# A two-layer decoder trunk on one core: adding the last overflow tile of the last layer in PSUM, and a second norm without GpSimd

## The chip, the cores and the metric

One core of a Trainium2 chip runs the whole program. The metric is the device time of one execution in microseconds, the median of several runs; lower is better.

## What is computed

Two layers over 512 positions of width 1024, batch 1. Each layer mixes the positions (layer 0 with a gated recurrence and a state-space model, layer 1 with two kinds of attention), normalises, sends every position to two of 16 SwiGLU experts, and normalises again. The change touches what stands at the end of each layer:

```python
x = layer_norm(DN_ALPHA * x + mix, ln1_g[layer], ln1_b[layer])
ffn = hier_moe(x, ...)        # sum over two experts e of gate[t, e] * expert_e(x[t])
x = layer_norm(DN_ALPHA * x + ffn, ln2_g[layer], ln2_b[layer])

def layer_norm(x, g, b):
    mu = mean(x, axis=-1); var = mean(square(x - mu), axis=-1)
    return (x - mu) * rsqrt(var + 1e-5) * g + b
```

The input and the result are 512 x 1024 float32.

## The kernel before

Tokens are rows, in four blocks of 128 partitions. The expert stage (`moe`, L1636) works on tiles of 128 tokens: one tile for each of the 16 experts, then up to NOV = 7 overflow tiles for experts that got more than 128 tokens. Every tile is gathered from the buffer `x1d` in memory (`gather`, L1571, an indirect DMA of GpSimd), goes through the expert's two products (`gate_up`, `hidden`, `hiddenT`, `down`), is scaled by its gate on ScalarE (L1616) and is added by a scattering DMA of GpSimd (L1617) to the buffer `yd` in memory, which starts as DN_ALPHA times x. Products in float32 are made of three products of rounded parts (`hilo`, L194 to L196: ScalarE writes the rounded part, VectorE the rest; `mm3`, L198 to L202).

Each of the seven overflow tiles stands in a branch, `with tc.If(nov > o)` (L1746). Every engine passes each branch by itself. On the way past a branch that isn't taken an engine only brings its semaphores up to where the branch would have left them; GpSimd does that with an instruction of its own for the semaphores of its DMAs (INC_SWDGE_SEM). With these inputs layer 0 takes four of the seven branches and layer 1 takes one.

After the branches the four blocks of 128 tokens of `yd` are read back on SyncE's queue (L1752) into `row` tiles. That read waits for the scatters and for GpSimd to be past all the branches. Then comes the second norm of the four blocks: `stats` on VectorE (L290, L1766), `scale` (the inverse root in some eleven tiny VectorE instructions for two blocks at a time, L266 to L281), and `norm`, which splits the columns: the lower 512 go through two VectorE instructions (L1782, L1784), the upper 512 through ScalarE (L1778), GpSimd (L1779, and L1781 for the first two blocks) and VectorE (L1787, for the last two). `weave` interleaves the generators, so the order on each engine is the order in which they are written. `finish` is called for each block: in layer 0 `odd_token` (L1289), which stores the block, transposes it on TensorE, splits it by `hilo` and multiplies it with the key and value weights of layer 1; in layer 1 only the DMA to the output (L1824).

Of the kernel before, what the change touches and what calls it, by code (L numbers as in the profile page):

```python
# [20 lines left out]
L = 512  # L21
# [141 lines left out]
class Trunk:  # L163
# [60 lines left out]
    def consts2(self):  # L224
        nc, c = self.nc, self.cst

        self.lt = c.tile([128, 128], BF, name="lt")
        self.iof = c.tile([128, 128], F32, name="iof")
        f = c.tile([128, 128], F32, name="ltf")
        nc.gpsimd.memset(f, 1.0)  # L230
        nc.gpsimd.affine_select(out=f, in_=f, compare_op=ALU.is_gt, fill=0.0, base=0,
                                pattern=[[1, 128]], channel_multiplier=-1)
        nc.gpsimd.tensor_copy(self.lt, f)
        self.onesf = c.tile([128, 128], F32, name="onesf")
        nc.gpsimd.memset(self.onesf, 1.0)
# [8 lines left out]
        nc.gpsimd.iota(bid, pattern=[[128, 4]], base=-8192, channel_multiplier=0,  # L244
                       allow_small_or_imprecise_dtypes=True)

        self.Q = c.tile([128, 8, 5], BF, name="Q")
# [15 lines left out]
        q.dma_start(bt, b.rearrange("(o d) -> o d", o=1).to_broadcast([128, D]))  # L263
        self.lnp = gt, bt

    def rsqrt_steps(self, z, var, n, pool, eps=1e-5):  # L266

        V = self.nc.vector
        t = lambda nm, dt=F32: pool.tile([128, n], dt, name="rq" + nm, bufs=4)
        h, m, y = t("h"), t("m"), t("i", I32)  # L270
        V.tensor_scalar(h, var, eps, 0.5, op0=ADD, op1=MUL)
        yield 1
        V.tensor_scalar(y, h.bitcast(I32), -0.5, float(0x5f3759df - 0x400000 - 0x80000000), op0=MUL, op1=ADD)
        y = y.bitcast(F32)
        for i in range(3):
            yield 1
            V.tensor_mul(m, y, y)
            yield 1
            V.tensor_mul(m, m, h)
# [763 lines left out]
    def wo_finish(self, layer, x):  # L1043
# [2 lines left out]
        V = nc.vector  # L1046
        res, mv, sts, rs = [], [], [], []
        for tt in range(NT):
            r = mo.tile([128, D], F32, name="row", bufs=6)
            if layer == 0:  # L1050
                nc.sync.dma_start(r, x[blk(tt), :])
            res.append(r)
# [550 lines left out]
        self.hilo(tp[:, :256], ht[:, 0], ht[:, 1])  # L1603
        return ht

    def down(self, s, ht, W):
        nc, mo = self.nc, self.mo
        ys = mo.tile([128, D], F32, name="row", bufs=6)
# [8 lines left out]
        return lambda: self.scattered(s, nc.gpsimd.indirect_dma_start(out=self.yd, out_offset=bass.IndirectOffsetOnAxis(ap=self.toki[:, s:s + 1], axis=0),  # L1617
                                     in_=ys, in_offset=None, bounds_check=L - 1, oob_is_err=False, compute_op=ADD))

    def after(self, inst, *before):  # L1620
        for b in before:
# [14 lines left out]
    def moe(self, layer, lg, between, start, before, after, finish):  # L1636
# [19 lines left out]
        def products(s, qs, xt):  # L1656
            nonlocal c, hp
            if qs[0] == 0:
                hp = self.acc()
            for q in qs:  # L1660
                self.gate_up(hp, xt, q, *self.chunk(c))
                c += 1
        hp = None
        products(0, (0, 1), xt)
        xn = self.xgT(ORD[1])
# [3 lines left out]
        for e in range(NEXP):  # L1669
# [78 lines left out]
        rows = []  # L1748
        mv = mo.tile([128, NT, 2], F32, name="bnmv4", bufs=1)
        for tt in range(NT):  # L1750
            r = mo.tile([128, D], F32, name="row", bufs=6)
# [4 lines left out]
        rs = mo.tile([128, NT], F32, name="lnrs", bufs=1)  # L1756
        nm = mo.tile([128, NT], F32, name="lnnm", bufs=1)
        g, b = self.lnp
        lo, hi = blk(0, 512), blk(1, 512)
        sts = [mo.tile([128, 2, 6], F32, name="bnst", bufs=4) for _ in range(NT)]  # L1760

        def stats(tt):
            for h in range(2):
                self.ln_stats(sts[tt], rows[tt], h)
                yield 1
            V.bn_aggr(mv[:, tt, :], sts[tt])  # L1766
            yield 1

        def scale(q):
            s = blk(q, 2)  # L1770
            yield from self.rsqrt_steps(rs[:, s], mv[:, s, 1], 2, mo)
            yield 1
            V.scalar_tensor_tensor(nm[:, s], mv[:, s, 0], -1.0, rs[:, s], op0=MUL, op1=MUL)
            yield 1

        def norm(tt):
            r = rows[tt]
            nc.scalar.activation(r[:, hi], r[:, hi], AF.Identity, scale=rs[:, tt:tt + 1], bias=nm[:, tt:tt + 1])  # L1778
            nc.gpsimd.tensor_mul(r[:, hi], r[:, hi], g[:, hi])  # L1779
            if tt < 2:  # L1780
                nc.gpsimd.tensor_add(r[:, hi], r[:, hi], b[:, hi])  # L1781
            V.scalar_tensor_tensor(r[:, lo], r[:, lo], mv[:, tt, 0:1], g[:, lo], op0=SUB, op1=MUL)  # L1782
            yield 1
            V.scalar_tensor_tensor(r[:, lo], r[:, lo], rs[:, tt:tt + 1], b[:, lo], op0=MUL, op1=ADD)  # L1784
            yield 1
            if tt >= 2:
                V.tensor_add(r[:, hi], r[:, hi], b[:, hi])  # L1787
            finish(tt, r)
            yield 1

        def each(f, *i):
            for j in i:
                yield from f(j)
        run_all(each(stats, 0, 1))
        weave(each(stats, 2, 3), scale(0))
        weave(each(norm, 0, 1), scale(1))
        run_all(each(norm, 2, 3))

    def run(self):
        nc, tc, I = self.nc, self.tc, self.I  # L1800
# [4 lines left out]
        for layer in range(2):  # L1805
# [5 lines left out]
            with ExitStack() as em:  # L1811
                self.mo = em.enter_context(tc.tile_pool(name="mo", bufs=2))
                self.rx = em.enter_context(tc.tile_pool(name="rxp", bufs=4))
                self.xg = []
                for i in range(4):
                    self.xg.append(self.mo.tile([128, D], F32, name=f"xg{i}", bufs=1))
                st.ahead_load = 4
# [41 lines left out]
```

## Time and profile before

| | us |
|---|---|
| median of 3 runs | 1006.04 (1003.46 to 1008.68) |
| the profiled execution, its own time | 1003.56 |
| its span in the profile | 1001.9 |
| TensorE matmul busy | 845.2 (84%) |
| VectorE busy | 789.1 (79%) |
| ScalarE busy | 566.4 (57%) |
| GpSimd busy | 311.9 (31%) |
| mean granted TensorE clock | 0.935 of full |

The profile is of one execution. Busy shares are means over stages with different limits: what counts for a change at the end of a layer is which wait ended last there. A line of a helper (L195, L196, L209) collects calls from many places, so that stretches of time and tiles have to be looked at.

### The profile page before, as it was taken

The page shows a single profiled execution, that of the slowest core. Times are in us where ns is not written, and L with a number is a line of the kernel's source. Part 1 is how long each engine was busy: PE and PEld are TensorE (multiplying, and loading weights), DVE is VectorE, ACT ScalarE, POOL GpSimd, SP SyncE. Part 2 cuts the span into 40 slices and gives each one's busy share as a digit, 9 for nine tenths or more (in the row PEclk, how much of TensorE's full clock was granted, in tenths as well). Part 3 has the DMA queues.
Part 4 walks back from the last instruction along what each step waited for, and adds up shares of the span by engine and source line. Part 5 has one row for each costly group of instructions (what it writes and reads, how often), then busy time and mean ns, then how long its engine had stood idle before and what let it go on. Part 6 is the DMA issues. An engine that isn't in the chain of part 4 may idle for free.

```text
span 1001.9 us, 13169 instructions
## 1 busy us (share of the span) xinstructions
PE 845.2 (84%) x4396; PEld 707.5 (71%) x4396; DVE 789.1 (79%) x1542; ACT 566.4 (57%) x922; POOL 311.9 (31%) x342
## 2 busy tenths in 40 slices
PE   5996999998975899999782899999993889999840
PEld 4895887787864788887661787788883668888630
DVE  6998668668679799997776657888788879999737
ACT  3331445536124899988673256656611688999721
POOL 6397971101102223222222302345611122232203
PEclk9998999999987999999995999989997799999975
DMA  9321112102947789999955350420093879999722
GB/s 280 123 93 43 43 43 95 43 1 61 358 174 260 296 299 365 371 375 305 322 177 191 105 127 1 120 50 2 4 365 140 327 251 337 361 382 362 239 65 114
DMA packets 52875, 192.05 MB, mean 192 GB/s; under 512 B 13492, under 2 KB 15552, under 8 KB 38336
## 3 DMA queue, kind: packets, MB, share of 16 engines
q1 hardware_dynamic: 37344, 156.47, 42.5%
q0 software_dynamic: 13440, 24.17, 9.2%
q10 hardware_dynamic: 2016, 10.49, 2.7%
q8 instruction: 38, 0.62, 0.2%
q14 instruction: 37, 0.30, 0.1%
HBM read 183.20 MB, written 31.98 MB: 215 GB/s over the span
## 4 chain that ended last, share of the span: by engine, by line
PE 47%; issue 15%; DVE 14%; DMA 12%; ACT 5%; POOL 5%; another core or an unknown queue 1%; ACTq 0%; SPq 0%; POOLq 0%; DVEq 0%
PE acc L200 10%; PE acc L202 10%; PE acc L201 10%; DMA yd<-row,r 8%; PE tp L209 2%; DVE u L196 2%; POOL yd L1617 2%; ACT u L195 1%; DMA xg<-x1d,r 1%; PE tp L1410 1%; POOL xg L1574 1%; DMA row<-yd 1%; PE sd L201 1%; PE sd L200 1%; POOL row L1779 1%
## 5 line engine op out<-in xcount | busy, mean ns | idle before, releaser
L200 PE MATMUL acc<-u 128*128 128x512 f32 (+1 forms) x712 | 296.5, 416 | 6.9 <-ACT u L195 6.9
L202 PE MATMUL acc<-u 128*128 128x512 f32 (+1 forms) x712 | 282.6, 397 | 5.5 <-DVE u L196 5.4
L201 PE MATMUL acc<-u 128*128 128x512 f32 (+1 forms) x712 | 281.7, 396 | 3.4 <-POOL u L196 1.9
L196 DVE TENSOR_TENSOR u<-u 128x1024 fp32r<-128x1024 f32 x142 | 172.2, 1241 | 27.0 <-ACT u L195 25.9
L195 ACT CAST u<-u 128x1024 fp32r<-128x1024 f32 x150 | 152.9, 1051 | 41.4 <-PE acc L202 36.6
L196 DVE TENSOR_TENSOR u<-rx,u 128x1024 fp32r<-128x1024 f32 x128 | 152.3, 1220 | 28.9 <-ACT u L195 27.8
L202 PEld LDWEIGHTS acc<-u 128*128 128x128 f32 x712 | 141.5, 199 | 35.6 <-DVE u L196 8.4
L200 PEld LDWEIGHTS acc<-u 128*128 128x128 f32 x712 | 143.8, 202 | 29.9 <-ACT u L195 8.7
L201 PEld LDWEIGHTS acc<-u 128*128 128x128 f32 x712 | 142.7, 200 | 25.8 <-DVE u L196 3.4
L1617 POOL DMA_INDIRECT yd<-row,r x37 | 58.8, 1588 | 239.1 <-ACT row L1616 186.8
L195 ACT CAST u<-rx 128x1024 fp32r<-128x1024 f32 x128 | 129.3, 1049 | 3.0 <-issue 1.8
L195 ACT CAST u<-tp 128x512 fp32r<-128x512 f32 x102 | 60.4, 608 | 72.0 <-PE tp L209 68.1
L196 DVE TENSOR_TENSOR u<-tp,u 128x512 fp32r<-128x512 f32 x102 | 67.8, 698 | 16.7 <-ACT u L195 16.6
L1574 POOL DMA_INDIRECT xg<-x1d,r x41 | 46.6, 1137 | 76.3 <-PE tp L209 66.2
L209 PE MATMUL tp<-idf,xg 128*128 128x128 f32 x312 | 49.9, 301 | 16.0 <-DMA xg<-x1d,r 9.8
L1400 POOL TENSOR_SCALAR P<-P,st 128x256 f32<-128x256 f32 (+3 forms) x32 | 35.1, 1097 | 90.3 <-DVE st L1376 55.2
L209 PEld LDWEIGHTS tp<-idf,xg 128*128 128x128 f32 x312 | 47.2, 208 | 21.3 <-issue 10.1
L200 PE MATMUL acc<-u,ht 128*128 128x512 f32 x148 | 58.5, 395 | 4.0 <-ACT ht L195 4.0
L202 PE MATMUL acc<-u,ht 128*128 128x512 f32 x148 | 57.7, 390 | 0.0
L201 PE MATMUL acc<-u,ht 128*128 128x512 f32 x148 | 57.6, 389 | 0.0
L1616 ACT ACTIVATE row<-acc,r 128x512 f32<-128x512 f32 x74 | 47.8, 687 | 10.0 <-PE acc L202 10.0
L1118 ACT COPY u<-tp 128x512 f32<-128x512 f32 x16 | 9.4, 587 | 66.3 <-PE tp L1117 56.3
(394 smaller groups left out, 1439.4 us busy)
## 6 DMA issues: line engine op xcount, KB each, us to landing
rx<-in_moe_w_gate_up_dram SPq DMA_DIRECT2D x48, 1024.0 KB, 10.8
u<-in_moe_w_gate_up_dram SPq DMA_DIRECT2D x24, 1024.0 KB, 16.2
u<-in_moe_w_down_dram SPq DMA_DIRECT2D x19, 1024.0 KB, 14.9
rx<-in_moe_w_down_dram SPq DMA_DIRECT2D x16, 1024.0 KB, 11.9
u<-in_ev_w_in_dram SPq DMA_DIRECT2D x10, 1024.0 KB, 6.2
u<-in_ev_w_out_dram SPq DMA_DIRECT2D x4, 1024.0 KB, 5.1
x1d<-row POOLq DMA_DIRECT2D x8, 512.0 KB, 5.6
yd<-row ACTq DMA_DIRECT2D x8, 512.0 KB, 3.6
```

Source lines behind the costliest of these rows:

```text
L195: self.nc.scalar.copy(hi, src)
L196: (self.nc.gpsimd if pool else self.nc.vector).tensor_sub(lo, src, hi)
L200: nc.tensor.matmul(ps, ah, bh, start=start, stop=False)
L201: nc.tensor.matmul(ps, ah, bl, start=False, stop=False)
L202: nc.tensor.matmul(ps, al, bh, start=False, stop=stop)
L209: self.nc.tensor.transpose(tp[:, blk(j)], src[:, s], self.idf)
L1400: nc.gpsimd.tensor_scalar(P[:, 1, :W], P[:, 1, :W], st[:, 5, 1:2], None, op0=MUL)
L1410: nc.tensor.transpose(tp[:, blk(2 * b + x)], P[:, x, blk(b0 + b)], self.idf)
L1574: nc.gpsimd.indirect_dma_start(out=xg, out_offset=None, in_=self.x1d, in_offset=bass.IndirectOffsetOnAxis(ap=self.toki[:, s:s + 1], axis=0 ...
L1616: nc.scalar.activation(ys[:, blk(c, 512)], yp[c], AF.Copy, scale=self.gate[:, s:s + 1])
L1617: return lambda: self.scattered(s, nc.gpsimd.indirect_dma_start(out=self.yd, out_offset=bass.IndirectOffsetOnAxis(ap=self.toki[:, s:s + 1] ...
L1779: nc.gpsimd.tensor_mul(r[:, hi], r[:, hi], g[:, hi])
```

## The change

In layer 1 (`stay`), an overflow tile's result is written to one fixed tile `ylast` and not scattered at once; if a further overflow tile follows, the scatter is issued at that one's start. So the last overflow tile never goes to memory. Its token numbers are kept as floats (`tok`, converted by GpSimd). At the end, for each block of 128 tokens, TensorE adds in PSUM the block as read from `yd` (identity times the float32 row) and the part of `ylast` that belongs to it (a 0/1 matrix `oh`, made by comparing token numbers, times the two rounded parts of `ylast`). The second norm of layer 1 reads these PSUM sums: blocks 0 and 1 with VectorE statistics, blocks 2 and 3 with sums accumulated by ScalarE. In layer 0 the blocks still come from `yd`; the norm there no longer uses GpSimd nor the split of the columns: VectorE does whole rows of 1024, and ScalarE the statistics of blocks 2 and 3. The `row` pool has five buffers instead of six in layer 1. The cut diff:

```diff
-    def rsqrt_steps(self, z, var, n, pool, eps=1e-5):
+    def rsqrt_steps(self, z, var, n, pool, eps=1e-5, of=1):
...
+            if n == 1 and self.fuse:
+                V.scalar_tensor_tensor(m, y, h, y, op0=MUL, op1=MUL)
+            else:
+                V.tensor_mul(m, y, y)
+                yield 1
+                V.tensor_mul(m, m, h)
...
+    def scatter(self, s, ys):
+        return self.scattered(s, self.nc.gpsimd.indirect_dma_start(out=self.yd, ..., in_=ys, ..., compute_op=ADD))
...
+            if e == 1 and stay:
+                nc.gpsimd.memset(ylast, 0.0)
+                nc.gpsimd.memset(tok, -1.0)
...
+            if o and stay:
+                self.scatter(s - 1, ylast)
...
-            self.down(s, ht, lambda k: (Wd[k][:, 0], Wd[k][:, 1]))()
+            scatter = self.down(s, ht, lambda k: (Wd[k][:, 0], Wd[k][:, 1]), ylast if stay else None)
+            if stay:
+                nc.gpsimd.tensor_copy(tok, self.toki[:, s:s + 1])
+            else:
+                scatter()
...
+        def sums(tt):
+            nc.scalar.activation(self.xg[tt - 2], rows[tt], AF.Identity, accum_out=sm[:, tt:tt + 1])
+        def means():
+            V.tensor_scalar(nm[:, 2:4], sm[:, 2:4], -1.0 / D, None, op0=MUL)
+        def squares(tt):
+            nc.scalar.activation(self.xg[tt - 2], rows[tt], AF.Square, bias=nm[:, tt:tt + 1], accum_out=ss[:, tt:tt + 1])
...
         def norm(tt):
             r = rows[tt]
-            nc.scalar.activation(r[:, hi], r[:, hi], AF.Identity, scale=rs[:, tt:tt + 1], bias=nm[:, tt:tt + 1])
-            nc.gpsimd.tensor_mul(r[:, hi], r[:, hi], g[:, hi])
-            if tt < 2:
-                nc.gpsimd.tensor_add(r[:, hi], r[:, hi], b[:, hi])
-            V.scalar_tensor_tensor(r[:, lo], r[:, lo], mv[:, tt, 0:1], g[:, lo], op0=SUB, op1=MUL)
-            V.scalar_tensor_tensor(r[:, lo], r[:, lo], rs[:, tt:tt + 1], b[:, lo], op0=MUL, op1=ADD)
-            if tt >= 2:
-                V.tensor_add(r[:, hi], r[:, hi], b[:, hi])
-            finish(tt, r)
+            m, op = (mv[:, tt, 0:1], SUB) if tt < 2 else (nm[:, tt:tt + 1], ADD)
+            V.scalar_tensor_tensor(r, r, m, g, op0=op, op1=MUL)
+            V.scalar_tensor_tensor(r, r, rs[:, tt:tt + 1], b, op0=MUL, op1=ADD)
+        if layer == 0:
+            stats(0)
+            run_all(scale(0, 1))
+            norm(0)
+            stats(1)
+            finish(0, rows[0])
+            sums(2)
+            sums(3)
+            run_all(scale(1, 2))
+            means()
+            norm(1)
+            squares(2)
+            squares(3)
+            run_all(scale(2, 4))
+            finish(1, rows[1])
+            for tt in (2, 3):
+                norm(tt)
+                finish(tt, rows[tt])
+        else:
+            V.tensor_scalar(t4, self.b128, -1.0, tok, op0=MUL, op1=ADD)
+            V.tensor_tensor(oh, ..., op=ALU.is_equal)
+            for c in range(2):
+                self.hilo(ylast[:, blk(c, 512)], y[:, 0, blk(c, 512)], y[:, 1, blk(c, 512)])
+            S = [[f() for _ in range(2)] for f in (self.sd, self.tp, self.acc, self.acc)]
+            def own(tt):
+                for c in range(2):
+                    nc.tensor.matmul(S[tt][c], self.idf, rows[tt][:, blk(c, 512)], start=True, stop=False)
+            def add(tt):
+                for c in range(2):
+                    for i in range(2):
+                        nc.tensor.matmul(S[tt][c], oh[:, tt, :], y[:, i, blk(c, 512)], start=False, stop=i == 1)
...
+            self.fuse = True
+            for tt in range(NT):
+                own(tt)
+                add(tt)
+            for tt in (2, 3):
+                for c in range(2):
+                    nc.scalar.activation(rows[tt][:, blk(c, 512)], S[tt][c], AF.Identity, accum_out=sh[:, tt, c:c + 1])
+            bn(0)
+            run_all(scale(0, 1))
+            bn(1)
+            passes(0, scale(1, 2))
+            for tt in (2, 3):
+                x = slice(tt, tt + 1)
+                V.tensor_scalar(nm[:, x], sh[:, tt, 0:1], sh[:, tt, 1:2], -1.0 / D, op0=ADD, op1=MUL)
+                squares(tt)
+            passes(1, iter(()))
+            run_all(scale(2, 4))
+            for tt in (2, 3):
+                norm(tt)
+                finish(tt, rows[tt])
```

`bn(tt)` takes the statistics of S[tt] on VectorE; `passes(tt, z)` applies the two steps of the norm to S[tt], the first in halves, with the tiny instructions of z between them, and sends the block out.

How the rows stand on the engines, at three places. First GpSimd in layer 1, at the first overflow branch (L1746 before, L1771 now). Before:

```order
L1746 COMPARE_AND_BRANCH
L1574 DMA xg_7211<-x1d,r_7616 128x1024
L1617 DMA yd<-row,r_7616 512x1024
L1746 UNCONDITIONAL_BRANCH
L1746 ISA
```

Now:

```order
L1771 COMPARE_AND_BRANCH
L1582 DMA xg_7212<-x1d,r_7617 128x1024
L1765 CAST ltok_7733<-r_7617 128x1
L1771 UNCONDITIONAL_BRANCH
L1771 ISA
L1771 UNCONDITIONAL_BRANCH
L1771 COMPARE_AND_BRANCH
L1615 DMA yd<-ylast,r_7617 512x1024
```

The scatter of the tile, which waited for ScalarE's result and held GpSimd before the other branches, is gone from the first branch and stands in the second, which isn't taken here; in its place is a conversion of 128 numbers.

Second, VectorE in layer 0, from the end of the first statistics on. Before:

```order
L1766 BN_AGGR bnmv_5243<-bnst 128x2
L290 BN_STATS bnst<-row 128x6
L271 TENSOR_SCALAR rqh<-bnmv_5243 128x2
L290 BN_STATS bnst<-row 128x6
L273 TENSOR_SCALAR rqi<-rqh 128x2
```

Now, from the end of the second block's inverse root (lnsm and lnss are ScalarE's sums):

```order
L289 SCALAR_TENSOR_TENSOR lnrs<-rqm,lnrs 128x1
L1798 TENSOR_SCALAR lnnm<-lnsm 128x2
L1813 SCALAR_TENSOR_TENSOR row<-row,bnmv_5245,lng 128x1024
L1814 SCALAR_TENSOR_TENSOR row<-row,lnrs,lnb 128x1024
L276 TENSOR_SCALAR rqh<-lnss 128x2
```

Before, the four statistics came first and the inverse roots were done for two blocks at a time between them; now each of the first two blocks goes through on its own, and whole rows of 1024 stand where halves of 512 stood.

Third, TensorE after the last branch of layer 1, where nothing stood before. Now:

```order
L1771 UNCONDITIONAL_BRANCH x2
L1849 MATMUL sd<-row,idf 128x512 x2
L1854 MATMUL sd<-u 128x512 x4
L1849 MATMUL tp<-row,idf 128x512 x2
L1854 MATMUL tp<-u 128x512 x4
```

Two float32 products with the identity and four products with the 0/1 matrix for each block; blocks 2 and 3 follow in the same way into `acc`.

## Rows read from the trace of the kernel before

**Rows 1.** The chain of waits at the end of layer 1: start us, length us, what.

```profile
966.35 5.34 another core or an unknown queue
```

**Rows 2.** Line L1746, us 900 to 1002: count, duration ns min/median/max, first and last start.

```profile
L1746 SPq EVENT_SEMAPHORE  x17: 17/17/17, 938.6 to 952.0; - x17
...
L1746 PEldq EVENT_SEMAPHORE  x6: 51/51/51, 963.3 to 967.3; - x6
...
L1746 ACTq EVENT_SEMAPHORE  x6: 17/17/17, 964.0 to 965.5; - x6
L1746 POOLq INC_SWDGE_SEM  x6: 775/784/821, 964.5 to 971.0; - x6
```

**Rows 3.** Layer 1's end in order of time: start us, length us, engine, line, operation.

```profile
962.65 1.37 ACT L1616 ACTIVATE row<-acc,r 128x512 f32<-128x512 f32 x2 [0.54 <-PE acc L202]
...
971.92 1.76 SPq L1752 DMA_DIRECT2D row<-yd  x4
975.21 1.29 DVE L290 BATCH_NORM_STATS2 bnst<-row 128x6 f32<-128x512 f32 x2 [11.66 <-DMA row<-yd]
...
978.56 0.69 DVE L290 BATCH_NORM_STATS2 bnst<-row 128x6 f32<-128x512 f32 x1 [0.43 <-DMA row<-yd]
...
997.51 0.68 DVE L1787 TENSOR_TENSOR row<-row,lnb 128x512 f32<-128x512 f32 x1
```

**Rows 4.** Layer 0's end in order of time, same columns.

```profile
535.97 1.29 DVE L290 BATCH_NORM_STATS2 bnst<-row 128x6 f32<-128x512 f32 x2 [1.79 <-DMA row<-yd]
...
545.32 1.23 DVE L273 TENSOR_SCALAR rqi<-rqh 128x2 int32<-128x2 int32 x1
...
566.90 1.29 DVE L196 TENSOR_TENSOR u<-tp,u 128x512 fp32r<-128x512 f32 x2 [1.11 <-ACT u L195]
```

**Rows 5.** Stretches: us, PE, PEld, DVE, ACT, POOL busy, granted clock, DMA share, GB/s.

```profile
580.00:600.00 20.00, 20.00 (x90) 16.57 (x89) 11.68 (x13) 10.48 (x14) 0.00 (x0) 1.00 0.59 144
949.00:952.00 3.00, 2.12 (x5) 1.42 (x6) 3.00 (x4) 3.00 (x4) 0.73 (x1) 0.73 1.00 157
952.00:955.00 3.00, 3.00 (x11) 2.36 (x10) 3.00 (x4) 1.18 (x2) 0.00 (x0) 0.70 0.28 49
967.00:968.00 1.00, 0.00 (x0) 0.00 (x0) 0.00 (x0) 0.00 (x0) 0.00 (x0) 0.71 0.12 25
```

**Rows 6.** Tile xg, us 940 to 1002: the gather of GpSimd and its landing.

```profile
L1574 POOL DMA_INDIRECT xg<-x1d,r x1: 1061/1061/1061, 948.7 to 948.7; - x1
...
DMA to landing us min/median/max: 5.8/5.8/5.8
```

**Rows 7.** DMA, us 952 to 954: GpSimd's queue, packets, MB, share of 16 engines.

```profile
q0 software_dynamic: 192, 0.13, 38.8%
```

**Rows 8.** Line L1746, us 965.6 to 966.6: a branch of TensorE's queue.

```profile
L1746 PEldq COMPARE_BRANCH  x1: 2004/2004/2004, 964.9 to 964.9; - x1
```

**Rows 9.** TensorE in order of time, around us 67, 91 and 952.

```profile
67.34 1.93 PE L935 MATMUL tp<-EP,BB 128*32 128x128 f32 x16
...
91.30 0.79 PE L979 MATMUL sd<-EP,H 128*128 128x128 f32 x2 [6.17 <-DVE H L969]
...
951.61 0.63 PE L201 MATMUL acc<-u 128*128 128x512 f32 x1
952.03 0.63 PE L202 MATMUL acc<-u 128*128 128x512 f32 x1
```

**Rows 10.** Groups by line and shape: engine, operation, count | busy us, mean ns | idle before.

```profile
L293 DVE SCALAR_TENSOR_TENSOR row<-row,bnmv,lng 128x1024 f32<-128x1024 f32 x8 | 10.2, 1275 | 0.0
...
L290 DVE BATCH_NORM_STATS2 bnst<-row 128x6 f32<-128x512 f32 x32 | 21.6, 687 | 15.1 <-DMA row<-yd 14.6
...
L1079 DVE SCALAR_TENSOR_TENSOR row<-row,acc 128x512 f32<-128x512 f32 x8 | 5.5, 688 | 10.1 <-PE acc L202 10.1
...
L281 DVE SCALAR_TENSOR_TENSOR rqy<-rqm,rqy 128x1 f32<-128x1 f32 x16 | 2.5, 159 | 0.6
...
L1386 ACT ACTIVATION_READ_ACCUMULATOR P<-acc,st 128x1 f32 x64 | 12.9, 202 | 0.0
```

More of the change, by code (lines that the diff above doesn't have):

```diff
@@ L245, in consts2 @@
                        allow_small_or_imprecise_dtypes=True)
+        self.b128 = c.tile([128, 4], F32, name="b128")
+        nc.gpsimd.tensor_scalar(self.b128, bid, 8192.0, None, op0=ADD)
         self.Q = c.tile([128, 8, 5], BF, name="Q")
@@ L1048, in wo_finish @@
         for tt in range(NT):
-            r = mo.tile([128, D], F32, name="row", bufs=6)
+            r = mo.tile([128, D], F32, name="row", bufs=self.nrow)
             if layer == 0:
@@ L1604, in hiddenT, with down @@
         return ht
-    def down(self, s, ht, W):
+    def scatter(self, s, ys):
+        return self.scattered(s, self.nc.gpsimd.indirect_dma_start(out=self.yd, out_offset=bass.IndirectOffsetOnAxis(ap=self.toki[:, s:s + 1], axis=0),
+                                                                   in_=ys, in_offset=None, bounds_check=L - 1, oob_is_err=False, compute_op=ADD))
+    def down(self, s, ht, W, ys=None):
         nc, mo = self.nc, self.mo
-        ys = mo.tile([128, D], F32, name="row", bufs=6)
+        ys = mo.tile([128, D], F32, name="row", bufs=self.nrow) if ys is None else ys
         yp = [self.acc() for _ in range(2)]
@@ L1616, in down @@
             nc.scalar.activation(ys[:, blk(c, 512)], yp[c], AF.Copy, scale=self.gate[:, s:s + 1])
-        return lambda: self.scattered(s, nc.gpsimd.indirect_dma_start(out=self.yd, out_offset=bass.IndirectOffsetOnAxis(ap=self.toki[:, s:s + 1], axis=0),
-                                     in_=ys, in_offset=None, bounds_check=L - 1, oob_is_err=False, compute_op=ADD))
+        return lambda: self.scatter(s, ys)
     def after(self, inst, *before):
@@ L1662, in products @@
                 c += 1
+        stay = layer == 1
+        if stay:
+            ylast = mo.tile([128, D], F32, name="ylast", bufs=1)
+            tok, t4 = [mo.tile([128, n], F32, name=f"ltok{n}", bufs=1) for n in (1, NT)]
         hp = None
@@ L1750, in moe @@
         for tt in range(NT):
-            r = mo.tile([128, D], F32, name="row", bufs=6)
+            r = mo.tile([128, D], F32, name="row", bufs=self.nrow)
             self.after(nc.sync.dma_start(r, self.yd[blk(tt), :]), *self.sc[-4:])
@@ L1755, in moe @@
         V = nc.vector
-        rs = mo.tile([128, NT], F32, name="lnrs", bufs=1)
-        nm = mo.tile([128, NT], F32, name="lnnm", bufs=1)
         g, b = self.lnp
-        lo, hi = blk(0, 512), blk(1, 512)
-        sts = [mo.tile([128, 2, 6], F32, name="bnst", bufs=4) for _ in range(NT)]
+        t = lambda nm: mo.tile([128, NT], F32, name=nm, bufs=1)
+        rs, sm, ss = t("lnrs"), t("lnsm"), t("lnss")
+        nm = t("lnnm")
         def stats(tt):
+            s = mo.tile([128, 2, 6], F32, name="bnst", bufs=4)
@@ L1763, in stats @@
             for h in range(2):
[L1764 to L1774, printed above, removed]
+                self.ln_stats(s, rows[tt], h)
+            V.bn_aggr(mv[:, tt, :], s)
@@ new lines, in stats, with scale @@
+            return mv[:, tt, 0:1], SUB
+        def sums(tt):
[4 more added lines that the diff above has]
+            nc.scalar.activation(self.xg[tt - 2], rows[tt], AF.Square, bias=nm[:, tt:tt + 1], accum_out=ss[:, tt:tt + 1])
+        def scale(a, z):
+            s = slice(a, z)
+            if a < 2:
+                yield from self.rsqrt_steps(rs[:, s], mv[:, s, 1], z - a, mo)
+            else:
+                yield from self.rsqrt_steps(rs[:, s], ss[:, s], z - a, mo, of=D)
@@ L1785, in norm @@
-            yield 1
-            if tt >= 2:
-                V.tensor_add(r[:, hi], r[:, hi], b[:, hi])
-            finish(tt, r)
[L1789 to L1797, printed above, removed]
+            m, op = (mv[:, tt, 0:1], SUB) if tt < 2 else (nm[:, tt:tt + 1], ADD)
+            V.scalar_tensor_tensor(r, r, m, g, op0=op, op1=MUL)
@@ new lines, in norm, with first_pass, second_pass, bn @@
+            V.scalar_tensor_tensor(r, r, rs[:, tt:tt + 1], b, op0=MUL, op1=ADD)
[17 more added lines that the diff above has]
+                finish(tt, rows[tt])
+        else:
+            y = self.unit(F32R).rearrange("p (s f) -> p s f", s=2)
+            oh = self.unit4()[:, :, 0:128]
+            V.tensor_scalar(t4, self.b128, -1.0, tok, op0=MUL, op1=ADD)
+            V.tensor_tensor(oh, self.iof.unsqueeze(1).to_broadcast([128, NT, 128]), t4.unsqueeze(2).to_broadcast([128, NT, 128]),
+                            op=ALU.is_equal)
+            for c in range(2):
+                self.hilo(ylast[:, blk(c, 512)], y[:, 0, blk(c, 512)], y[:, 1, blk(c, 512)])
+            S = [[f() for _ in range(2)] for f in (self.sd, self.tp, self.acc, self.acc)]
+            sh = mo.tile([128, NT, 2], F32, name="lnsh", bufs=1)
+            def own(tt):
[5 more added lines that the diff above has]
+                        nc.tensor.matmul(S[tt][c], oh[:, tt, :], y[:, i, blk(c, 512)], start=False, stop=i == 1)
+            def first_pass(tt, c):
+                V.scalar_tensor_tensor(rows[tt][:, blk(c, 512)], S[tt][c], mv[:, tt, 0:1], g[:, blk(c, 512)], op0=SUB, op1=MUL)
+            def second_pass(tt):
+                V.scalar_tensor_tensor(rows[tt], rows[tt], rs[:, tt:tt + 1], b, op0=MUL, op1=ADD)
+                finish(tt, rows[tt])
+            def bn(tt):
+                s = mo.tile([128, 2, 6], F32, name="bnst", bufs=4)
+                for h in range(2):
+                    V.bn_stats(s[:, h, :], S[tt][h])
+                V.bn_aggr(mv[:, tt, :], s)
+            def passes(tt, z):
+                for c in range(2):
+                    first_pass(tt, c)
+                    for _ in range(3):
+                        next(z, None)
+                second_pass(tt)
+                run_all(z)
+            self.fuse = True
[3 more added lines that the diff above has]
+            for tt in (2, 3):
+                for c in range(2):
+                    nc.scalar.activation(rows[tt][:, blk(c, 512)], S[tt][c], AF.Identity, accum_out=sh[:, tt, c:c + 1])
[11 more added lines that the diff above has]
+                norm(tt)
+                finish(tt, rows[tt])
@@ L1813, in run @@
                 self.rx = em.enter_context(tc.tile_pool(name="rxp", bufs=4))
+                self.fuse = False
                 self.xg = []
+                self.nrow = 6 - layer
                 for i in range(4):
```

9 lines of the change are left out of this document (4 added, 5 removed).

## The prediction

> **What bounds the kernel now.** The page's share by engine says little here: TensorE is busy 84% of the span, but the change lies in two stretches where it stands idle or starves. So I read first the chain of waits at the end of layer 1. There the read of `yd` waits 5.34 us for something the profile can't name [rows 1]. The listing of the branch line names it: SyncE is past all branches at 952.0, ScalarE at 965.5, TensorE at 967.3, but GpSimd's six INC_SWDGE_SEM run from 964.5 to 971.0, at 0.78 us each [rows 2]. They stand behind the last scatter on GpSimd's queue, and that waits for ScalarE's result, whose last two pieces start at 962.65. So the read is issued at 971.92, its first block is in use at 975.21, its last at 978.56, and VectorE then works to 998.19 [rows 3]. The span ends 3.7 us later, after the last store. In layer 0 the order of time shows the same norm from 535.97 to 568.19, and in it tiny VectorE instructions of 1.23 us [rows 4], which stand beside GpSimd's products; the usual one takes 0.16 [rows 10]. Afterwards TensorE is busy for the whole of the stretch 580 to 600 at full clock [rows 5], so what layer 0's end gains is carried to the end of the program.
>
> **Layer 1, what is removed.** The last scatter goes, and GpSimd reaches the untaken branches after the gather, which ends at 949.7 and lands 5.8 us after its start, at 954.5 [rows 6]. The earlier scatters have landed by then: its queue's packets end about 953 [rows 7]. The new conversion of 128 numbers I take at 0.2 us. Six branches at 0.78 plus some 0.3 between, two of them after that landing, end near 958. The read is issued there and its blocks land 3.3 to 6.6 us later (the spacing in rows 3), by 965. All of this now lies beside the expert's own work; if that cover failed, up to 9 us would come back. The next to be late is TensorE: it is through its branches only at 967.35, since one of them took 2.0 us [rows 8].
>
> **Layer 1, what is added.** ScalarE and VectorE split `ylast` from 965.5 on: two casts, each at most the 0.69 of a piece of L1616 [rows 3], and, after the 0/1 matrix, two subtractions of 0.7, ready at 968 or 969, while TensorE still does the first identity products. Those are in float32, of which no 512-wide one stands in the trace. The nearest are the 16 records of L935 in 1.93 us, 128 columns each [rows 9]. The step is (1.93 - 0.27) / 15 = 0.11; eight products of the program make these 16 records, so one costs 0.22 us and one of 512 columns 0.88. The lower bound is 0.45: two records at the 0.22 us per 512 columns that 90 matmuls in 20.00 us give [rows 5]. I take 0.88, since those are float32 too and 32 weight columns can't hold them up. At half clock it doubles to 1.76, and a rounded product takes 0.42, the step of L201 to L202 at 951.6 [rows 9]. The clock decides: it falls at about 967.4 after TensorE's last matmul at 963.3 (the mean of 967 to 968 is 0.71 [rows 5]). So I start at half clock, and let it come back after 3.4 us: the slow stretch around 952 lasted that long ((0.27 + 0.30) x 3 / 0.5, from the means 0.73 and 0.70 of rows 5). The first block's own part ends at 970.9, the sum S[0] stands at 972.0, and the others follow every 2 x 0.88 + 4 x 0.22 = 2.65 us, to 979.95.
>
> VectorE's queue from 972.0, prices of rows 10 with 0.035 us between dependent instructions: statistics of a block 2 x 0.66 + 0.21 = 1.53, an inverse root of 8 fused tiny ones 1.56 (11 unfused ones 2.15), a half-row step 0.72, a whole-row step 1.32. Block 0's statistics and root end at 975.1, block 1's statistics at 976.6, block 0's steps with block 1's root between them (1.44 + 1.56 + 1.32) at 981.0. Then VectorE must wait for ScalarE's sums of block 3: 979.95 plus two of 0.7 with the 0.20 read of the accumulator [rows 10] is 981.8, and the means end at 982.0. Block 1's steps (2.76) end at 984.8. ScalarE's squares, a whole row at 1.37 + 0.20 each, lie beside them and end at 984.9. Root 2.15, four whole-row steps 5.28: 992.2, against 998.19. **Layer 1 gains 5.9 us.** By the lower price of the identity products it gains 8.0, because S[3] then stops being waited for; at half clock all the way S[3] is 988.4 and VectorE ends at 1000.6, a loss of 2.4.
>
> Eight VectorE instructions now read PSUM instead of SBUF. In the trace that makes no difference: 688 ns for the PSUM step L1079, 687 for statistics from SBUF [rows 10]; so I add nothing. [...]
>
> **Layer 0.** VectorE's new queue holds two statistics 3.06, three roots 6.45, the means 0.2, eight whole-row steps 10.56 and eight subtractions of 0.7, together 25.9 us. Waits come on top for blocks 2 and 3 only, since behind blocks 0 and 1 other VectorE work follows: four transposes of 128 columns, 0.45 us at L935's step and 0.9 at half clock, and ScalarE's cast of at most 0.69, some 1.35 a block. 535.97 + 25.9 + 2.7 = 564.6 against 568.19: **3.6 us gained**. Without any wait it would be 6.3; with the key products of the last block at half clock (24 of 256 columns, at half of 0.42 instead of half of 0.22) it would be 1.2. ScalarE's sums and squares end before VectorE asks for them.
>
> **The rest.** Five `row` buffers instead of six: a buffer comes back after five experts of 36 products at 0.22 us, 40 us, by which its scatter has landed: nothing, or the excess if one took longer. The memset of `ylast`, about as long as ScalarE's 1.37 for a whole row, falls while GpSimd waits for the next tile's result: nothing; without that cover its 1.4. The constant `b128` is one tiny instruction early. SyncE's queue only gets its reads earlier.
>
> Sum: -5.9 - 3.6 = -9.5, so the profiled execution's 1003.56 becomes 994.1. The median of the runs shown is 2.5 higher, 1006.04; from it the same gain gives 996.5, which I forecast. Half a per cent, 5 us, is about what a measurement of this kernel can tell from no change.
>
> **The rivals.**
> *A stall at the way out of the branches.* Before, GpSimd's 971.78 hid what the other engines did there; now a second 2.0 us like TensorE's in rows 8, on VectorE or ScalarE behind TensorE's, is exposed: 998.5. For it: that one record. Against: ScalarE passed its six in 1.5 us [rows 2]. [...]
> *Layer 0 gains nothing,* if the halves of blocks waited for TensorE and ScalarE anyway: 1000.1. For it: half clock there; against: the queue sum above.
> *The read is not freed,* so that the change doesn't do what it says: GpSimd's branches wait for something that ends with the tile. The blocks then land at 975.2 as before, S[0] stands at about 978 to 979.2 and VectorE ends 20.2 later, 998.2 to 999.4: layer 1 loses up to 1.2, in all 1003 to 1004. Against: both landings of rows 6 and 7.
> *TensorE at half clock throughout the tail:* +2.4 - 3.6, 1004.8. Against: around 952 the clock came back while TensorE was less busy than it would be here.
> *The float32 identity products are far dearer* (slower). Place: TensorE after the branches. Price: the pair of L979 at 91.30 takes 0.79 us after an idle stretch [rows 9]; read as 0.395 a record of 128 columns it makes 3.16 for one of 512 columns, 25.3 for eight, and with 16 at 0.42 S[3] stands at 999.6. VectorE ends 12.3 after it, 1011.9: +13.7 - 3.6, so 1016. It decides from S[3] later than 989.5, an identity product of about 1.9 us. Against: L935.
>
> **How the numbers follow.** Forecast 0.50, stall 0.14, layer 0 nothing 0.12, read not freed 0.08, half clock 0.11, dear products 0.05. Faster by over 0.5%: the first three, less a slip below 1001, and the chance of a partly freed read: 0.77. Within: 0.18. Slower: 0.05. The range runs from 990.5 (both lower bounds, gains 8.0 and 6.3, would give 991.7, and the runs differ by 2.6 around their median) to 1002.5, past the stall and layer 0 and part of the way to the others; about 0.2 is left out.
>
> **What would show it.** Right: the last read of `yd` issued near 958 beside the last tile's products; no DMA between ScalarE's last piece of `ylast` and VectorE's statistics; TensorE's first identity product at 967 to 968, some 1.8 us long, at half clock; layer 0's norm 28 to 29 us long with no tiny instruction over 0.3 us. Wrong: a read later than 965, an identity pair over 3 us, VectorE idle over 2 us between its first statistics in layer 1 and its last step, or matmuls at half clock after 975.

## The result and the profile after

| | before | changed |
|---|---|---|
| median, us | 1006.9 (4 runs, 1003.46 to 1008.68) | 992.92 (4 runs, 992.3 to 995.26) |
| ratio to before | | 0.9869, 95% interval 0.9837 to 0.9902 |
| span of the profiled execution | 1001.9 | 993.6 |
| layer 0's second norm: start of the first statistics to the end of VectorE's last split of a block | 32.22 | 27.96 |
| layer 1's tail: start of ScalarE's last two pieces to VectorE's end | 35.54 | 29.29 |

The ratio is 13.2 us of 1006.9 (9.9 to 16.4); 9.5 had been forecast. The profiled execution of the changed kernel is the slowest of its four (995.26) and that of the kernel before (1003.56) is among the fastest of its, so the two spans stand only 8.3 us apart.

First, layer 1's end in order of time (start us, length us, engine, line, operation), the changed kernel; it answers to [rows 3]:

```profile
955.01 1.76 SPq L1777 DMA_DIRECT2D row<-yd  x4
960.61 1.33 ACT L1628 ACTIVATE ylast<-acc,r 128x512 f32<-128x512 f32 x2 [0.62 <-PE acc L202]
963.40 0.23 DVE L1839 TENSOR_SCALAR ltok<-b,ltok 128x4 f32<-128x4 f32 x1 [1.96 <-DVEq L1771]
966.12 0.69 DVE L1840 TENSOR_TENSOR u<-iof,ltok 128x512 fp32r<-128x512 f32 x1 [2.48 <-PEq L1771]
966.50 3.72 PE L1849 MATMUL sd<-row,idf 128*128 128x512 f32 x4 [5.29 <-PEq L1771]
966.63 1.14 ACT L195 CAST u<-ylast 128x512 fp32r<-128x512 f32 x2 [4.69 <-PEq L1771]
...
970.72 1.29 DVE L1865 BATCH_NORM_STATS2 bnst<-sd 128x6 f32<-128x512 f32 x2 [2.15 <-PE sd L1854]
970.99 1.88 PE L1849 MATMUL tp<-row,idf 128*128 128x512 f32 x4
...
979.96 0.21 DVE L1889 TENSOR_SCALAR lnnm<-lnsh 128x1 f32<-128x1 f32 x1 [0.43 <-ACT row L1881]
980.09 1.40 DVE L1857 SCALAR_TENSOR_TENSOR row<-tp,bnmv,lng 128x512 f32<-128x512 f32 x2
...
988.62 1.28 DVE L1814 SCALAR_TENSOR_TENSOR row<-row,lnrs,lnb 128x1024 f32<-128x1024 f32 x1
```

The reads of `yd` are issued from 955.01, while the last tile is still being worked on. What is late now is in the brackets: TensorE, ScalarE and VectorE all wait for "PEq L1771", TensorE's own way past the untaken branches. The branch line L1771 by engine, us 890 to 994 (count, duration ns min/median/max, first and last start), answers to [rows 2, 8]:

```profile
L1771 SPq EVENT_SEMAPHORE  x17: 17/17/17, 935.9 to 950.0; - x17
...
L1771 PEldq COMPARE_BRANCH  x8: 70/214/2932, 940.0 to 966.1; - x8
...
L1771 POOLq INC_SWDGE_SEM  x6: 755/772/791, 946.9 to 954.2; - x6
L1771 PEldq EVENT_SEMAPHORE  x6: 51/51/51, 961.3 to 966.4; - x6
L1771 DVEq EVENT_SEMAPHORE  x6: 21/21/21, 961.5 to 963.3; - x6
L1771 ACTq EVENT_SEMAPHORE  x6: 17/17/17, 962.0 to 963.4; - x6
```

GpSimd's six instructions cost what they did, but end at 955 instead of 971.8. VectorE and ScalarE are past at 963.4, TensorE only at 966.5, since one of its branches took 2.93 us. The granted clock falls in that gap (columns as in [rows 5]):

```profile
960.00:963.00 3.00, 1.22 (x6) 0.64 (x4) 1.44 (x2) 1.33 (x2) 0.00 (x0) 1.00 0.63 246
963.00:964.00 1.00, 0.00 (x0) 0.00 (x0) 0.23 (x1) 0.00 (x0) 0.00 (x0) 0.62 0.16 37
...
968.00:970.00 2.00, 2.00 (x4) 0.67 (x2) 0.57 (x1) 0.00 (x0) 0.00 (x0) 0.50 0.00 0
970.00:971.00 1.00, 1.00 (x6) 0.78 (x5) 0.28 (x1) 0.00 (x0) 0.00 (x0) 0.97 0.00 0
```

So the first two identity products (shown as two records each, x4) take 3.72 us at half clock, and the next two 1.88 as listed, with a step of 0.86 a product, at full clock. Layer 0's end, VectorE in order of time, answers to [rows 4]:

```profile
537.83 1.29 DVE L298 BATCH_NORM_STATS2 bnst<-row 128x6 f32<-128x512 f32 x2 [1.83 <-DMA row<-yd]
...
554.05 1.28 DVE L196 TENSOR_TENSOR u<-tp,u 128x512 fp32r<-128x512 f32 x2
...
559.27 1.29 DVE L196 TENSOR_TENSOR u<-tp,u 128x512 fp32r<-128x512 f32 x2 [1.43 <-ACT u L195]
```

No wait stands ahead of the second block's split, and 1.43 us ahead of the third's; the fourth's, at 564.50, has 1.43 too and ends at 565.79.

In the old norm of layer 0 (the kernel before, start us, length us as above) some of VectorE's instructions are slow beside GpSimd's:

```profile
550.45 1.81 POOL L1779 TENSOR_TENSOR row<-row,lng 128x512 f32<-128x512 f32 x1 [2.58 <-ACT row L1778]
551.03 1.25 DVE L279 TENSOR_TENSOR rqm<-rqm,rqh 128x2 f32<-128x2 f32 x1
563.54 1.65 DVE L1784 SCALAR_TENSOR_TENSOR row<-row,lnrs,lnb 128x512 f32<-128x512 f32 x1
```

With the one in [rows 4], three tiny ones take 1.22 to 1.25 us where the others take 0.16 or less, and one step of half a row takes 1.65 where the others take 0.75: 4.1 us together more than these, and each of the four begins while GpSimd has a product or a sum of half a row running (1.68 to 1.81 us each). In the new norm no tiny one takes over 0.3 us. That is nearly the whole gain of layer 0's norm, but no run takes GpSimd alone out of the old norm, so what its absence gives and what the new order gives isn't shown apart.

### The profile page after: what moved, and what is told of

Same layout as the page of the kernel before. It is cut to its first block, busy times and chain, and to the rows that moved or that the text cites. A ratio compares the mean times of both kernels' runs of the same rounds, so it can differ in the third digit from the quotient of the medians.

```text
span 993.6 us, 13230 instructions
## 1 busy us (share of the span) xinstructions
PE 859.7 (87%) x4428; PEld 714.5 (72%) x4428; DVE 789.4 (79%) x1547; ACT 571.9 (58%) x936; POOL 292.1 (29%) x333
## 5 line engine op out<-in xcount | busy, mean ns | idle before, releaser
L201 PEld LDWEIGHTS acc<-u 128*128 128x128 f32 x712 | 142.7, 200 | 25.9 <-DVE u L196 3.4
```

The source lines that it names most:

```text
L201: nc.tensor.matmul(ps, ah, bl, start=False, stop=False)
```

## The experiments

Theory A: the two stretches are the whole gain, and the two parts add up. Theory B: some 3 us come from a third place, since 13.2 is more than 4.3 + 6.2. All are timed against the kernel before.

| run | median us | ratio (95% interval) | layer 0's norm | layer 1's tail |
|---|---|---|---|---|
| changed, second time | 992.11 | 0.9862 (0.9830 to 0.9895) | 27.96 | 28.51 |
| layer 0's part alone | 999.81 | 0.9936 (0.9912 to 0.9961) | 27.96 | 36.23 |
| layer 1's part alone | 997.25 | 0.9920 (0.9890 to 0.9950) | 32.23 | 28.57 |
| through memory, new norm in both | 995.64 | 0.9892 (0.9865 to 0.9919) | 27.96 | 31.98 |
| changed, one branch | 988.15 | 0.9840 (0.9811 to 0.9868) | 27.95 | 22.45 |
| before, one branch | 1000.2 | 0.9959 (0.9941 to 0.9977) | 32.46 | 32.10 |
| changed, two branches | 987.11 | 0.9823 (0.9795 to 0.9851) | 27.95 | 23.91 |
| two branches, order of the tail | 988.2 | 0.9841 (0.9811 to 0.9871) | 27.96 | 23.77 |
| before, against itself | 1004.38 | 1.0010 (0.9992 to 1.0028) | 32.37 | 36.54 |
| changed, third time | 992.78 | 0.9896 (0.9878 to 0.9914) | 27.97 | 29.34 |

The last two columns are the two stretches of the first table, in us, each from that run's one profile.

**The changed kernel again** (no edit).

> The changed kernel as it is, timed again in five rounds beside the kernel before, and profiled once more. Theory A (the two stretches are all): the two profiles differ by 4.3 us in layer 0's norm (32.2 to 28.0) and by 6.2 us in the tail of layer 1 (34.9 to 28.7), together 10.5 us; the ratio then comes out near 0.990 (996 against 1006.5). Theory B (there is a third gain outside the two norms, about 3 us): the ratio stays near 0.987, and the profile shows a stretch between the two norms that is shorter than before in both profiles of the changed kernel.

The ratio stayed at 0.986, near B's 0.987, but B's sign is missing: from the end of layer 0's norm to ScalarE's last two pieces it is 394.8 and 395.6 us in the two profiles of the changed kernel, and 394.5 before. What differs is where layer 0's norm began: at 537.83 in the first profile of the changed kernel, at 535.36 in this one and at 535.97 before.

**Each part alone.** For layer 0's part, layer 1 got back the way through memory, six `row` buffers and, in place of the sums in PSUM, the split norm:

```diff
-        stay = layer == 1
+        stay = False
...
         else:
+            run_all(each(stats0, 0, 1))
+            weave(each(stats0, 2, 3), scale0(0))
+            weave(each(norm0, 0, 1), scale0(1))
+            run_all(each(norm0, 2, 3))
```

For layer 1's part, these four lines stand in layer 0's place and `stay` is left as it is.

> Layer 0's new norm alone; layer 1 is as before (last overflow tile through memory, split columns with GpSimd, six row buffers). Theory A: -4.3 us, ratio 0.996, and layer 1's tail as before, 34.9 us from TensorE's last product to VectorE's last step. Theory B with the third gain in layer 0's neighbourhood: -7 us, ratio 0.993. Rival (layer 0 gains nothing, its gain given back later): 0, ratio 1.000.

> Layer 1's part alone: the last overflow tile is added in PSUM, layer 0's norm is as before with GpSimd. Theory A: -6.2 us, ratio 0.994, a tail of 28.7 us from TensorE's last product to VectorE's last step. Theory B with the third gain in layer 1: -9 us, ratio 0.991. Rival (the two parts are not additive, since what layer 0 gains moves layer 1's transfers): this run and layer 0's run alone do not add up to the whole within 2 us.

The product of the two ratios is 0.9857, against 0.9862 for both together: the parts add up. Each part's time lies between theory A's and theory B's, with both in its interval, so the profiles decide, for A: the stretch that has the change is as in the changed kernel, and the other as in the kernel before. By the profiles layer 0's part is 4.4 us (a mean of 32.32 in the four profiles with the old norm, 27.95 to 27.97 in all eight with the new), layer 1's 7.2 (means of 36.10 of three and 28.93 of four). The times gave 6.4 and 8.0, each with its interval of some 2.5 to 3 either way around it; the sum of the stretches, 11.5, lies in the intervals of all three measurements of the changed kernel.

**What the adding in PSUM is worth by itself.** Both layers have the norm without GpSimd, and the last tile goes through memory, with six `row` buffers in both layers, so that layer 0's branch of the code serves both:

```diff
-        stay = layer == 1
+        stay = False
...
-        if layer == 0:
+        if True:
```

> The last overflow tile of layer 1 goes through memory as before (scatter, read back, six row buffers), but both layers have layer 0's new norm without GpSimd. Theory A (each part has its own share of layer 1's gain): the blocks come at 975 as before, 11.7 us after TensorE's last product, VectorE's queue of statistics 3.06, roots 6.45, means 0.2 and eight whole-row steps 10.56 takes 20.3 instead of 23.0, so layer 1 gains 2.7 and the whole 7.0 us, ratio 0.993. Rival C (the way through memory is what costs, the norm gives nothing in layer 1): -4.3, ratio 0.996. Rival D (the norm is the whole gain of layer 1, the adding on chip gives nothing): -10.5, ratio 0.990.

By its ratio this is nearest to rival D, and A's 0.993 lies outside the interval. But D has the adding on chip give nothing, and the changed kernel, timed in the same rounds, is 3.5 us faster (992.11 against 995.64; its slowest run, 992.85, is just below the fastest here, 992.88). The profile too decides for A, with a larger share of the norm. The order of time at this kernel's layer 1 end:

```profile
959.95 1.37 ACT L1628 ACTIVATE row<-acc,r 128x512 f32<-128x512 f32 x2 [0.52 <-PE acc L202]
961.59 1.58 POOL L1615 DMA_INDIRECT yd<-row,r  x1 [14.46 <-ACTq L1771]
969.04 1.76 SPq L1777 DMA_DIRECT2D row<-yd  x4
972.36 1.29 DVE L298 BATCH_NORM_STATS2 bnst<-row 128x6 f32<-128x512 f32 x2 [11.49 <-DMA row<-yd]
```

The way through memory is as long as before, 12.4 us from ScalarE's pieces to the statistics (12.56 in [rows 3]); VectorE's end comes 19.6 us after that, where the old norm took 23.0 to 23.9 in three profiles. So, by the one profile of this kernel, of layer 1's 7.2 us the norm without GpSimd is 4.1 (36.10 to 31.98), and PSUM, with its own order of the norm, 3.1 (31.98 to 28.93). The larger part is not the one that the change is about.

**What bounds the tail now: fewer branches.** In the changed kernel and in the one before, for layer 1 only:

```diff
-        for o in range(NOV):
+        for o in range(NOV if layer == 0 else 1):
             with tc.If(nov > o):
```

> The changed kernel with only the first of the seven overflow branches written in layer 1 (it leaves out the tiles that a second to seventh overflow would need; with these inputs there is one, so all work that ran before still runs). In the profile of the changed kernel the first identity product waits 4.7 us after TensorE's last product for six untaken branches: five of 0.38 us with their semaphores and one whose branch instruction takes 2.4 us. Theory A (that one is a part of the way past the branches, and goes with them): the first identity product starts within 0.4 us of the last product or of the blocks' landing, VectorE's statistics 4 to 5 us earlier; 988 us, 4.5 below the changed kernel. Rival (the code behind the branches has to be fetched in any case, so a stall of 2 to 3 us stays at the way out): 990.5, and the gap on TensorE is 2.4 us or more. Rival 2 (the blocks of yd land later than TensorE is free, since GpSimd's read comes no earlier): the gap ends with a DMA of row<-yd.

> The kernel before with only the first of the seven overflow branches written in layer 1 (it leaves out the tiles that a second to seventh overflow would need; with these inputs there is one). Theory A (the way through memory cost 11.7 us between TensorE's last product and the first statistics, of which GpSimd's six branches were the last part): the read is released by the landing of the scatter, some 2 us after its issue ends at 965.9, instead of by GpSimd at 971.8; the tail is 4 to 5 us shorter, 1001 us, ratio 0.9955. Then what the change gained in layer 1 is mostly the freeing of the read from GpSimd, and a kernel without those branches would have had it without PSUM. Rival (the scatter's landing itself takes until 971): no gain, ratio 1.000.

The changed kernel with one branch, order of time:

```profile
958.75 1.32 ACT L1628 ACTIVATE ylast<-acc,r 128x512 f32<-128x512 f32 x2 [0.62 <-PE acc L202]
959.19 1.88 PE L1849 MATMUL sd<-row,idf 128*128 128x512 f32 x4
...
961.90 1.30 DVE L1865 BATCH_NORM_STATS2 bnst<-sd 128x6 f32<-128x512 f32 x2
```

and its branch line:

```profile
L1771 PEldq COMPARE_BRANCH  x2: 70/120/169, 938.2 to 956.8; - x2
```

TensorE's first identity product follows the last product of the tile at once, no branch of its takes over 0.17 us, the clock stays at 1.00 (granted, 955 to 963), and the same two products take 1.88 us instead of 3.72. The tail is 6.5 us shorter than the mean of 28.93, where A had 4 to 5 for TensorE's way alone: the half clock goes with it. The stall doesn't stay at the way out, so it belongs to passing the untaken branches; this edit takes away both the branches and the code that they jump over, and doesn't tell which of the two it is. In the kernel before the same edit gave 3.4 to 4.4 us of the tail: the scatter is issued at 968.28 for 1.58, the read at 972.71, 2.85 us behind the end of that (6.05 in the kernel before, from 965.87 to 971.92), and GpSimd's branches no longer stand between. So both ways of adding pay for the branches, at different engines: GpSimd's before, TensorE's now.

**A version that keeps all seven slots.** In layer 1 the first overflow tile has a branch, the other six share one:

```diff
-        for o in range(NOV):
-            with tc.If(nov > o):
-                state = overflow(o, *state)
+        for z in ([(o,) for o in range(NOV)] if layer == 0 else [(0,), range(1, NOV)]):
+            with tc.If(nov > z[0]):
+                for o in z:
+                    state = overflow(o, *state)
```

> The changed kernel with two branches in layer 1 instead of seven: the first overflow tile in one, the second to the seventh together in the other (slots without tokens have indices out of bounds and a gate of zero, so they add nothing; with these inputs that second branch isn't taken). Theory A (the 2.4 us stall belongs to passing many branches): TensorE waits 0.4 us instead of 4.7, 988.5 us. Rival (one jump past a long body stalls as long as the worst of six): the wait is 2.8 us, 990.5. Rival 2 (GpSimd's one untaken branch now brings up six times as many semaphores, as long as before): the read is issued no earlier.

This is faster than both kernels, 987.11 us, and the slowest of its runs (987.41) is below the fastest of the changed kernel's (991.41). Those two weren't timed in the same rounds; the kernel before was at 1004.35 in these and at 1003.6 to 1006.9 in the others. Order of time, and TensorE's branches:

```profile
960.22 1.96 PE L1850 MATMUL sd<-row,idf 128*128 128x512 f32 x4 [1.69 <-PEq L1771]
...
962.67 1.30 DVE L1866 BATCH_NORM_STATS2 bnst<-sd 128x6 f32<-128x512 f32 x2 [0.39 <-PE sd L1855]
```

```profile
L1771 PEldq COMPARE_BRANCH  x3: 70/169/3834, 938.5 to 956.2; - x3
L1771 POOLq INC_SWDGE_SEM  x1: 799/799/799, 949.5 to 949.5; - x1
```

The one untaken branch takes 3.83 us, more than the 2.93 of the worst of six above, as the rival said; but it begins at 956.2, while products are still running to 958.5, so only 1.69 us is waited for, and the first two identity products take 1.96 us, near the 1.88 at full clock and far from the 3.72 at half. The wait is neither theory A's 0.4 nor the rival's 2.8. GpSimd's single instruction costs as much as each of the six did, and the read is issued at 950.27, so rival 2 fell. Where a layer has more than one overflow tile but fewer than seven, this version would work through empty ones; no run here shows that price.

**Order of the tail**, on top of the two branches:

```diff
             for tt in range(NT):
-                own(tt)
-                add(tt)
+                for cs in ((0,), (1,)) if tt == 0 else ((0, 1),):
+                    own(tt, cs)
+                    add(tt, cs)
...
+            center(2)
+            first_pass(1, 0)
+            center(3)
...
+            for c in range(2):
+                x = blk(c, 512)
+                V.scalar_tensor_tensor(rows[3][:, x], rows[3][:, x], rs[:, 3:4], b[:, x], op0=MUL, op1=ADD)
+                (nc.scalar, nc.sync)[c].dma_start(self.out[0, blk(3), x], rows[3][:, x])
```

> As the kernel with two branches, and three changes of order in layer 1's tail: the first sum is finished for its lower half before its upper half is begun, VectorE takes the mean of block 3 between the two first steps of block 1 (the changed kernel's trace shows 0.42 us of waiting there), and the last step and the last store are made in halves on two queues. Theory: 0.6 from the first, 0.4 from the second, 0.6 from the third (the last store moves 512 KB in some 1.2 us), so 1.6 below the kernel with two branches and some 987 us in all. Rival: VectorE's queue isn't what sets the end, since TensorE's last sum is waited for; then only the 0.6 of the store.

A miss for two of three terms. VectorE's end stands 23.77 us after ScalarE's pieces, against 23.91: the first half's statistics start sooner (4.1 us after the pieces, against 4.7) and the second half's then wait 0.62 for TensorE. From VectorE's end to the end of the span it is 3.1 instead of 3.8, so the halved store gives its 0.6. The amount is the rival's, but not its reason: no wait for TensorE's last sum stands in VectorE's queue. The times (988.2 and 987.11) don't tell the two versions apart.

**Straying.**

> The kernel before, timed against itself and profiled once more. It tells how far the times of one kernel stray and which stretches stray. Theory A (the change's gain is the two stretches, 4.3 and 7.0 us by the profiles so far, and what is over that in the ratio of 0.987 is straying of the runs of the kernel before): ratio within 0.3% of 1, layer 0's norm again 32.2 us, the stretch from VectorE's last split pair of weights to the end of the span again 40.7 us within 0.7, and a start of the first that differs by up to 3 us. Theory B (there is a third gain): all stretches are as in the first profile.

> The changed kernel a third time, on the same chip as the kernel before against itself. Theory A: some 11.3 us below the median of that one, ratio 0.989, with stretches of 28.0 and 33.7 to 34.5 us. Theory B: 13 us below again, ratio 0.987.

The kernel before against itself is 1.0010; its runs reach from 1000.0 to 1008.96 on that chip. In its second profile layer 0's norm was the same within 0.2 us and the stretch from the last split pair of weights to the end 41.6, 0.9 more and not within the 0.7 expected. The changed kernel's third measurement is A's: 10.4 us below (8.6 to 12.2). A third gain was not shown: with no part of the change ahead of it but one tiny constant, layer 0's norm began anywhere from 534.15 to 540.14 in the twelve profiles. The stretch between the two norms is, if anything, longer with the new norm in layer 0: 394.1 to 395.9 us in eight profiles (mean 395.1) against 393.3 to 394.5 in four (mean 394.0). About 1 us of layer 0's gain may be given back there; no run shows where.

## Why the prediction was right

The time, 992.92, lies in the range, 3.6 us below the 996.5 that I forecast. Term by term:

- **The read freed.** Right: the four reads are issued from 955.01 to some 956.8, beside the last tile; forecast 958, though my own terms (954.5, two branches of 1.08 and the conversion) add up to about 957. The whole tail stands 2 us earlier than before, so against ScalarE's pieces the first read is 5.6 us ahead where I had 4.7. The rival *read not freed* fell; by its own terms it stood for 1002.4 to 1003.6, not 1003 to 1004.
- **The price of the identity products.** Right: 0.86 at full clock where I took 0.88, 3.72 for two at half clock where I took 3.52. I had written that an identity pair over 3 us would show me wrong; that mark contradicted my own price at half clock and tells nothing. The rival *far dearer* fell.
- **The clock.** Right in what it cost, but in part by luck: I let it fall at 967.4, as the first identity product starts, and come back after 3.4 us. By the granted clock it was at half from 963.2 to 970.1 in the first profile, and from 964.0 to 967.4 in the second: it fell 2.0 and 4.5 us after TensorE's last product (4.1 in the kernel before), and was low for 6.8 and 3.4 us. What the sum needed, its return after the first identity product, came 3.6 and 3.15 us later. So *half clock throughout* fell. I took the fall as given; in the kernel with one branch it doesn't come.
- **TensorE's branches.** Undersized. I carried over the gap of [rows 3, 8], 4.06 us from the last product to 967.35; now it was 5.3, 4.7 and 5.3 in the three profiles, and one branch took 2.93 us in the first and 2.41 in the second, not 2.0. The rival *stall at the way out* wanted a second stall, on VectorE or ScalarE: it didn't come, both passed in 2 us. It was TensorE's own stall, already in my sum, that all three waited for, and it was not large enough to make the rival's time.
- **From TensorE's first identity product to VectorE's end.** Oversized by 1.4: I had 24.85 us, and it took 23.4. The first sum stood after 4.2 us (I had 4.65); VectorE's last root took 1.98 and its last four steps 5.12 (2.15 and 5.28), and it waited 0.43 for ScalarE's sums (0.8). The two slips nearly cancel: TensorE began 5.9 us after ScalarE's pieces and not 4.7.
- **Layer 0.** 4.3 to 4.4 gained, 3.6 forecast. The wait per late block was 1.43 (taken as 1.35) and the second block's didn't occur, as argued; the first block's took 0.49, which I had left out, and VectorE's queue without waits 24.6 instead of the 25.9 that I added up. *Layer 0 gains nothing* fell. That the gain is carried to the end whole, as I took it, isn't shown: about 1 us may be lost on the way (see Straying).
- **Layer 1.** 5.9 forecast; 6.2 between the first two profiles, 7.2 between the means of all. Of the difference of those two, 0.6 us is on the side of the old tail, 35.54 in the profile that I worked from and 36.23 and 36.54 in two others: its blocks land unevenly (the third waited for 0.43 in [rows 3], 1.31 in the second profile of the kernel before). The other 0.4 is on the new one, 29.29 in its first profile and 28.93 in the mean. That 6.2 came so near to 5.9 is in part luck, since the two slips above went opposite ways.

So the mechanism and the signs held; the sum was 9.5 where the two stretches show 11.5, and the first two ratios stood some 2 us above that again, which the third, 10.4, did not. What I didn't say, since I costed only the whole of layer 1: over half of its gain is the norm without GpSimd.

I added nothing for the eight VectorE instructions that now read PSUM. The statistics from PSUM took 1.29 us a pair (970.72 in the changed kernel), as from SBUF in [rows 3], and the steps of half a row from PSUM 0.75 (975.45), as from SBUF at 982.93 in the kernel before.

## What to carry to other kernels

Keeping a last partial sum on chip frees the read, but what is gained is only the distance to the next engine that is late: here from GpSimd's branches to TensorE's (3.1 us by one profile). Before building a way around memory, try the two cheap edits by themselves: an untangled norm (4.1 of 7.2 us) and fewer untaken branches at the end of the program (5.0 and 6.5 us of the changed kernel's tail, 3.4 to 4.4 of the old one), and put slots that are seldom used behind one branch. The two edits together, without PSUM, were not run, so what PSUM would add to them stays open.

## What was not expected of the hardware

- An untaken branch instruction took TensorE some 0.2 us (the median at the end of layer 1), but one of the six 2.00 us in the kernel before and 2.93 and 2.41 in the first two profiles of the changed one, and one jump past six tiles 3.83 and 3.62 in two profiles. In the 2.4 us of the changed kernel's second profile (961.3 to 963.7) nearly all that moved was on the queues that the profile calls instruction (packets, MB, share of 16 engines):

```profile
q8 instruction: 1, 0.02, 2.6%
q14 instruction: 2, 0.02, 2.3%
q1 hardware_dynamic: 2, 0.00, 0.0%
```

  These three packets of the two queues move in the first 0.7 us of the stall. In the first profile it is three again, in the first 0.7 of 2.93 us, and in the kernel before two, in the first 0.9 of 2.00; others move up to 1.4 us before or after it. In the changed kernel with one branch neither is there: no branch of TensorE's takes over 0.17 us, and these queues moved nothing from 955 to 962. That the stall waits for these packets is my guess; it lasts 1.2 to 2.3 us longer than they do, and no run changes them alone.
- The same GpSimd instruction, INC_SWDGE_SEM, takes 0.77 us per branch in layer 1 and 1.3 in layer 0 (medians of six and three, in the changed kernel); why was not tried.
- After a gap of 4.7 to 5.3 us on TensorE the first two identity products took 3.52 to 3.75 us in three profiles of the changed kernel, 1.6 to 1.9 more than the 1.88 at full clock; after a gap of 1.69 they took 1.96.
